# Both feed-forward up stages of a hybrid decoder layer: combined right blocks formed token-major in place, and the second norm's affine moved into the norm

## Chip, cores and metric

One core of a Trainium2 chip runs the whole layer. The metric is the device time of one execution in microseconds (us). The profile is of one execution; TensorE's clock is reported as a share of its full speed, the upper of its two levels (2.4 GHz); the other is 1.2 GHz.

## What is computed

The layer is a first feed-forward block (f1), a token mixer (retention and RWKV-7 heads), a second feed-forward block (f2) and a gated embedding, each of the first three followed by a residual sum and a layer norm. All of it is fp32, for 1024 tokens of width 1024; the hidden width D_FF is 2816.

```python
def _layer_norm(x, g, b):
    xf = x.astype(jnp.float32)
    mu = jnp.mean(xf, axis=-1, keepdims=True)
    var = jnp.mean(jnp.square(xf - mu), axis=-1, keepdims=True)
    y = (xf - mu) * lax.rsqrt(var + LN_EPS) * g.astype(jnp.float32) + b.astype(jnp.float32)
    return y.astype(x.dtype)

def _swiglu(x, w_gu, w_down):
    hdn = jnp.einsum('bsd,df->bsf', x, w_gu)
    gate, up = jnp.split(hdn, 2, axis=-1)
    return jnp.einsum('bsf,fd->bsd', jax.nn.silu(gate) * up, w_down)

x = _layer_norm(DEEPNORM_ALPHA * x + 0.5 * _swiglu(x, ffn1_w_gu[i], ffn1_w_down[i]), ln1_g[i], ln1_b[i])
mix = _token_mixer(x, w_in[i], ret_gn_g[i], ...)
x = _layer_norm(DEEPNORM_ALPHA * x + mix, ln2_g[i], ln2_b[i])
x = _layer_norm(DEEPNORM_ALPHA * x + 0.5 * _swiglu(x, ffn2_w_gu[i], ffn2_w_down[i]), ln3_g[i], ln3_b[i])
```

## The kernel before

An fp32 matrix product is made from three products of rounded parts: a `hi` part (a cast to fp32r on ScalarE, ACT, line L47) and a `lo` part (source minus hi, on VectorE, DVE, or GpSimd, POOL, line L48). `mm3` issues them as L61, L62 and L63.

**The up stage** (`ffn_up`) multiplies x by w_gu, which gives the gate and the up half (two *parts*). Tokens and features are halved, which gives two-by-two blocks, and each part of each hidden slice j = 0 to 10 takes seven block products m1 to m7 (the table `PRODUCTS`) in place of eight, of 12 matmuls of 128x512 each: 84 matmuls to a part, 168 to a slice. The left operands are combinations S1 to S4 of the weight blocks A11 to A22, made anew for each j in `ffn_w`: load (`f1w`, `f2w`, L100, on SyncE's DMA queue, SP), sums on DVE (L107), splits on ACT with DVE or POOL. The right operands are the token blocks B11, B21, B22 and their combinations T1 = B12 - B11, T3 = B22 - B12, T2 = B22 - T1, T4 = B21 - T2. They are made once, while slice j = 0 runs, and stay in SBUF for the ten slices after it.

The tokens lie token-major. A matmul wants them feature-major, so TensorE transposes them by 128x128 pieces (L229, into a PSUM tile `tp` of which there are two). Before, the four plain blocks are transposed (64 transposes to a stage). B11 and B21 are split straight from there (`first`). Of the other two, c and d (tiles called `pair`), ACT copies the transposed block to SBUF (`place`, L234; in f2 with the affine of the second norm, gain and bias as columns, L236), and then T1, T3, T2 and T4 are formed feature-major from SBUF (`sub` and `add`, L224 and L178) and split (`store`, L240 and L224), on DVE and POOL. In the code j = 0 is written out by hand, products in the order 1, 2, 5, 7, 6, 3, 4; the scheduler of the framework then sets each engine's order by priorities and dependences.

**Weights of the down stage.** `down_blocks` loads four blocks of w_down for one f (`f1tb`, `f2tb`, L146), subtracts on POOL (L148) and stores the four results to DRAM (`wt`, L149), where the down stage fetches them. A call after slice j handles f = j - 1; the call after j = 1 also handles f = 10. These loads and stores share SP's queue with the weight loads of the next slices, in order.

**The second norm.** The mixer's last step, `w_out_group`, adds its products into eight token tiles `xacc` (L1133, DVE). `layer_norm_stats` takes statistics on DVE (L507, L508, L510, L511) and normalises a tile in one ACT instruction (L513). The first four tiles (h = 0) are normalised at the end of the mixer (L1193), ahead of the last group (L1194), the other four (h = 1) when f2's j = 0 first asks for them (`load2`, L1406). Gain and bias are put on twice: by `place` and the split in f2's j = 0, and again token-major in `ffn_down` on the residual (`affine`, 16 DVE instructions of 128x1024, with gain and bias loaded as rows, 512 KB each).

Of the kernel before, what the change touches and what calls it, by code (L numbers as in the profile page):

```python
# [29 lines left out]
class Layer:  # L30
# [120 lines left out]
    def ffn_up(self, nm, X, xp, pool, pp, load, pair, release, w_gu, hd, hooks, w_down, wt, gb=None):  # L151
# [69 lines left out]

        tmp = lambda: pool.tile([P, HALF], F32, tag="s", name=f"{nm}t{self.uid()}", bufs=5)
        part = lambda n, k: (X[n][0][:, k], X[n][1][:, k])
        sub = lambda eng, o, a, b: eng.tensor_tensor(out=o, in0=a, in1=b, op=ALU.subtract)  # L224

        def transposed(half, h, k):
            ps = pp.tile([P, HALF], F32, tag="tp", name=f"{nm}tp{h}_{k}", bufs=2)
            for j in range(4):
                nc.tensor.transpose(ps[:, j * P:(j + 1) * P], half[j][:, k * P:(k + 1) * P], self.ident)  # L229
            return ps  # L230

        def place(dst, ps, k):
            if gb is None:
                nc.scalar.copy(dst, ps)  # L234
            else:
                nc.scalar.activation(dst, ps, AF.Identity, bias=gb[1][:, k:k + 1], scale=gb[0][:, k:k + 1])  # L236

        def store(n, k, src, eng, copy=None):
            hi, lo = part(n, k)
            (copy or nc.scalar.copy)(hi, src)  # L240
            sub(eng, lo, src, hi)

        def first(n, kh):
            for k in range(4):
                ps = transposed(half, 0, kh + k)
                if gb is None:
                    store(n, k, ps, V)
                else:
                    t = tmp()
                    place(t, ps, kh + k)  # L250
                    store(n, k, t, G_ if k % 2 else V, V.tensor_copy)

        with ExitStack() as c1, ExitStack() as c2:
            half = load(0, 0)
            s = [start(0, p_, None, None) for p_ in range(2)]
            stage = lambda: [next(p_.g) for p_ in s]
            load(0, 1)
            half1 = load(1, 0) if gb is None else None
            stage()
            if half1:  # L260
                load(1, 1)
            first("B11", 0)
            stage()
            first("B21", 4)
            b = {}
# [5 lines left out]
            if not half1:  # L271
                half1 = load(1, 0)
            c, d = zip(*[pair(k) for k in range(4)])
            early = xp.tile([P, 4, HALF], F32, tag="T4l", name=nm + "T2")
# [12 lines left out]
            for p_ in s:  # L287
                b[5, p_] = matmuls(p_, 5)
# [51 lines left out]
            for j in range(1, NJ):  # L340
# [14 lines left out]
                for f in (j - 1, NJ - 1)[:1 + (j == 1)]:  # L355
# [1112 lines left out]
```

## Time and profile before

| what | value |
|---|---|
| median of three runs | 2406.56 us (2405.73 to 2412.31) |
| the profiled execution's own time | 2407.18 us |
| its span | 2405.4 us |
| mean granted clock | 0.975 |
| PE busy | 2262.6 us, 94% of the span |
| DVE busy | 1667.1 us, 69% |
| ACT busy | 823.1 us, 34% |
| POOL busy | 839.0 us, 35% |
| DMA | 345.96 MB, mean 144 GB/s |
| chain that ended last | PE 73%, DVE 18%, DMA 3%, issue 3%, ACT 2%, POOL 1% |

The span is the profiled time without what lies around it (1.8 us here). A busy share is a mean over stages: PE is close to full in most of the program, and DVE's 69% is the mean of stretches in which it is idle half the time and others in which it never stops. "Chain" is the sequence of work that ended last, followed backwards through what released each step.

### The profile page before, as it was taken

How to read it: one execution, taken by the hardware profiler on the slowest of the kernel's cores; microseconds unless marked ns; L12 is line 12 of the kernel's file. 1: busy time of each engine (PE TensorE's matmuls, PEld its weight loads, DVE VectorE, ACT ScalarE, POOL GpSimd, SP SyncE). 2: the span in 40 equal slices, each digit the busy share in tenths (PEclk: the TensorE clock that was granted, in tenths of full speed). 3: DMA queues.
4: the chain of work that ended last, by engine and by line, in shares of the span. 5: the costliest groups of instructions: out<-in, count | busy, mean ns of one | idle time of the engine just before them, and what ended most of it. 6: DMA issues, size and time to landing. Idle time of an engine off the chain costs nothing.

```text
span 2405.4 us, 30769 instructions
## 1 busy us (share of the span) xinstructions
PE 2262.6 (94%) x10705; PEld 1809.2 (75%) x10705; DVE 1667.1 (69%) x2688; ACT 823.1 (34%) x1398; POOL 839.0 (35%) x642
## 2 busy tenths in 40 slices
PE   7999999999998999999899899978999999999989
PEld 5778888788776677777677677756888887787767
DVE  7776877656783378774864866688677766867862
ACT  4322332244532523322322323263223322445430
POOL 4754454200223333332533433257545443001330
PEclk9999999999998999999999999998999999999999
DMA  3545445397335442333333353224554543974321
GB/s 110 180 153 168 151 156 167 124 352 240 98 114 164 153 121 88 105 85 105 112 97 103 112 170 116 85 88 140 184 162 141 175 141 129 379 244 132 97 75 40
DMA packets 289841, 345.96 MB, mean 144 GB/s; under 512 B 35571, under 2 KB 162134, under 8 KB 289686
## 3 DMA queue, kind: packets, MB, share of 16 engines
q1 hardware_dynamic: 286128, 335.04, 43.5%
q0 software_dynamic: 2304, 8.39, 0.9%
q8 instruction: 84, 1.38, 0.2%
q10 hardware_dynamic: 1254, 0.58, 0.1%
q14 instruction: 71, 0.58, 0.1%
HBM read 237.50 MB, written 106.43 MB: 143 GB/s over the span
## 4 chain that ended last, share of the span: by engine, by line
PE 73%; DVE 18%; DMA 3%; issue 3%; ACT 2%; POOL 1%; SPq 1%; ACTq 0%; DVEq 0%; POOLq 0%
PE f2m L63 5%; PE f2m L62 5%; PE f2m L61 5%; PE f1m L61 5%; PE f1m L62 5%; PE f1m L63 5%; PE z L62 3%; PE z L61 3%; PE z L63 3%; PE f1qa L62 2%; PE f1qa L63 2%; PE f1qa L61 2%; PE scpw L1041 1%; DVE ixw L977 1%; DVE itw L975 1%
## 5 line engine op out<-in xcount | busy, mean ns | idle before, releaser
L63 PE MATMUL z<-x1Th,lo_win 128*128 128x512 f32 x448 | 189.2, 422 | 3.5 <-DVE lo_win L48 2.9
L61 PE MATMUL z<-x1Th,hi_win 128*128 128x512 f32 x448 | 188.9, 422 | 0.5 <-ACT hi_win L47 0.5
L62 PE MATMUL z<-x1Tl,hi_win 128*128 128x512 f32 x448 | 187.0, 417 | 0.0
L48 POOL TENSOR_TENSOR lo_win<-raw_win,hi_win 128x512 fp32r<-128x512 f32 x54 | 75.4, 1396 | 156.7 <-ACT hi_win L47 136.9
L975 DVE TENSOR_TENSOR itw<-iltw,ixw 32x31 f32<-32x31 f32 (+15 forms) x248 | 106.7, 430 | 28.8 <-DMA iltw<-scrw 13.4
L977 DVE TENSOR_TENSOR ixw<-ixw,itw 32x31 f32<-32x31 f32 (+15 forms) x248 | 109.7, 442 | 4.0
L63 PEld LDWEIGHTS z<-x1Th,lo_win 128*128 128x128 f32 x448 | 86.8, 194 | 23.3 <-DVE lo_win L48 3.8
L61 PEld LDWEIGHTS z<-x1Th,hi_win 128*128 128x128 f32 x448 | 86.6, 193 | 22.7 <-issue 3.6
L62 PEld LDWEIGHTS z<-x1Tl,hi_win 128*128 128x128 f32 x448 | 86.9, 194 | 19.8 <-issue 3.0
L148 POOL TENSOR_TENSOR f2tb<-f2tb,f2tb 128x512 f32<-128x512 f32 x44 | 68.3, 1553 | 76.6 <-DMA f2tb<-in_ffn_w_down 69.3
L148 POOL TENSOR_TENSOR f1tb<-f1tb,f1tb 128x512 f32<-128x512 f32 x44 | 67.1, 1526 | 70.5 <-DMA f1tb<-in_ffn_w_down 65.5
L48 DVE TENSOR_TENSOR f1hl<-f1s,f1hh 128x512 fp32r<-128x512 f32 x63 | 44.9, 713 | 61.4 <-ACT f1hh L47 59.8
L48 DVE TENSOR_TENSOR f2hl<-f2s,f2hh 128x512 fp32r<-128x512 f32 x63 | 44.7, 710 | 47.9 <-ACT f2hh L47 47.8
L107 DVE TENSOR_TENSOR f2S<-f2w 128x512 f32<-128x512 f32 x22 | 17.5, 794 | 82.2 <-DMA f2w<-in_ffn_w_gu 82.2
L62 PE MATMUL f2qa<-f2vl,f2hh 128*128 128x512 f32 x164 | 65.0, 397 | 3.6 <-DVE f2vl L48 3.6
L62 PE MATMUL f1qa<-f1vl,f1hh 128*128 128x512 f32 x164 | 64.6, 394 | 3.1 <-DVE f1vl L48 3.1
L47 ACT CAST f2hh<-f2s 128x512 fp32r<-128x512 f32 x63 | 39.2, 623 | 82.2 <-PE f2qb L62 35.3
L47 ACT CAST f1hh<-f1s 128x512 fp32r<-128x512 f32 x63 | 39.2, 622 | 80.7 <-PE f1qa L62 35.3
L47 ACT CAST hi_win<-raw_win 128x512 fp32r<-128x512 f32 x56 | 34.6, 618 | 93.8 <-PE z L62 83.6
L601 ACT COPY zs<-z 128x512 f32<-128x512 f32 x56 | 32.7, 583 | 95.6 <-PE z L63 80.2
L107 DVE TENSOR_TENSOR f1S<-f1w 128x512 f32<-128x512 f32 x22 | 16.2, 738 | 70.6 <-DMA f1w<-in_ffn_w_gu 60.6
L63 PE MATMUL f2qa<-f2vh,f2hl 128*128 128x512 f32 x164 | 64.5, 393 | 0.5 <-DVE f2hl L48 0.5
(791 smaller groups left out, 7314.9 us busy)
## 6 DMA issues: line engine op xcount, KB each, us to landing
f1w<-in_ffn_w_gu SPq DMA_DIRECT2D x44, 512.0 KB
f2w<-in_ffn_w_gu SPq DMA_DIRECT2D x44, 512.0 KB
f1s<-hd SPq DMA_DIRECT2D x63, 256.0 KB
f2s<-hd SPq DMA_DIRECT2D x63, 256.0 KB
zs<-zs SPq DMA_DIRECT2D x56, 256.0 KB
raw_win<-in_w_in SPq DMA_DIRECT2D x54, 256.0 KB
f1tb<-in_ffn_w_down SPq DMA_DIRECT2D x44, 256.0 KB
wt<-f1tb SPq DMA_DIRECT2D x44, 256.0 KB
```

What stands on the lines that cost most here:

```text
L47: self.last_split = self.nc.scalar.copy(hi, src).ins
L48: (eng or self.nc.vector).tensor_tensor(out=lo, in0=src, in1=hi, op=ALU.subtract)
L61: mm(ps, a[0], b[0], start=first, stop=False)
L62: mm(ps, a[0], b[1], start=False, stop=False)
L63: mm(ps, a[1], b[0], start=False, stop=last)
L107: sub = lambda o, a, b, op=ALU.subtract: V.tensor_tensor(out=o, in0=a, in1=b, op=op)
L148: nc.gpsimd.tensor_tensor(out=t, in0=a, in1=b, op=ALU.subtract)
L601: nc.scalar.copy(zs, ps)
L975: nc.vector.tensor_tensor(out=t, in0=lt[:, j, j + 1:].unsqueeze(2).broadcast_to([B, n, c]), in1=x[:, j:j + 1, 0:c].broadcast_to([B, n, c]) ...
L977: nc.vector.tensor_tensor(out=x[:, j + 1:, 0:c], in0=x[:, j + 1:, 0:c], in1=t, op=ALU.add)
L1041: nc.tensor.matmul(ps[e][:, 0:2 * P], kp[rr, cs], ar[rr, c].rearrange("p a t -> p (a t)"), start=True, stop=True)
```

## The change

In `ffn_up` the combinations are formed before the transposes, token-major and in place in the tiles that hold the tokens (a, b, c and d are the slices with B11, B12, B21 and B22): a becomes T1 = b - a on DVE, b becomes T3 = d - b on POOL, d becomes T2 = d - a on DVE once B22 has been transposed, and c becomes T4 = c - d on POOL. Each of the seven right blocks then goes through the new function `block`: 16 transposes, hi by ACT and lo by DVE, both straight from PSUM. That is 112 transposes to a stage for 64, no `pair`, and no affine in f2's up stage. The products are called in the order 1, 2, 5, 7, 6, 3, 4 as before. Over the program DVE has 2606 rows before and after, ACT 1411 and 1395, POOL 641 and 627, PE 8964 and 9060.

`layer_norm_stats` gets an optional pair of rows; with them it normalises and applies gain and bias in four DVE instructions of 128x512 to a tile (L471 and L476 in the new numbering) and no ACT one. All eight tiles go this way at the end of the mixer; the rows lie in two matrices of the mixer (`M1`) that are free by then. `ffn_down` loses its 16 affine instructions and two loads. `down_blocks` is called for f = j - 2, not after j = 1, and twice after j = 4 (f = 2 and 9) and j = 7 (f = 5 and 10).

```diff
@@ ffn_up
+        cut = lambda tiles, n: [t[:, n * HALF:(n + 1) * HALF] for t in tiles]
+        def subs(eng, out, x, y):
+            for o, p, q in zip(out, x, y):
+                eng.tensor_tensor(out=o, in0=p, in1=q, op=ALU.subtract)
+        def block(n, src):
+            for k in range(4):
+                ps = pp.tile([P, HALF], F32, tag="tp", name=f"{nm}tp{n}_{k}", bufs=2)
+                for i in range(4):
+                    nc.tensor.transpose(ps[:, i * P:(i + 1) * P], src[i][:, k * P:(k + 1) * P], self.ident)
+                self.split(X[n][0][:, k], X[n][1][:, k], ps)
...
-            for k in range(4):
-                place(c[k], transposed(half1, 1, k), k)
-                t = early[:, k]
-                sub(V, t, c[k], part("B11", k)[0])
-                sub(V, t, t, part("B11", k)[1])
-                store("T1", k, t, G_)
+            subs(V, a, b, a)
+            block("T1", a)
             for p_ in s:
-                b[2, p_] = matmuls(p_, 2)
-            for k in range(4):
-                place(d[k], transposed(half1, 1, 4 + k), 4 + k)
-            load(1, 2)
+                r[2, p_] = matmuls(p_, 2)
+            subs(G_, b, d, b)
             stage()
             for p_ in s:
-                b[5, p_] = matmuls(p_, 5)
+                r[5, p_] = matmuls(p_, 5)
+            block("T3", b)
+            stage()
+            block("B22", d)
+            for p_ in s:
+                r[7, p_] = matmuls(p_, 7)
+            subs(V, d, d, a)
+            block("T2", d)
+            subs(G_, c, c, d)
...
-            for k in range(4):
-                sub(V, c[k], d[k], c[k])
-                store("T3", k, c[k], V)
...
-            for k in range(4):
-                t = early[:, k]
-                sub(V, t, d[k], t)
-                store("T2", k, t, V)
             for p_ in s:
-                b[6, p_] = matmuls(p_, 6)
...
-                sub(G_, c[k], part("B21", k)[0], early[:, k])
...
-                add(c[k], c[k], part("B21", k)[1], V)
-                store("T4", k, c[k], G_)
+                r[6, p_] = matmuls(p_, 6)
+            block("T4", c)
...
-                for f in (j - 1, NJ - 1)[:1 + (j == 1)]:
+                for f in {1: (), 4: (2, 9), 7: (5, 10)}.get(j, (j - 2,)):
                     self.down_blocks(nm, w_down, wt, f, pool)
...
@@ ffn_down
-        def affine(t):
-            V.tensor_tensor(out=acc[t], in0=acc[t], in1=gb[1][0], op=ALU.mult)
-            V.tensor_tensor(out=acc[t], in0=acc[t], in1=gb[1][1], op=ALU.add)
...
@@ layer_norm_stats
+        if rows:
+            for i in range(2):
+                a = x[:, i * HALF:(i + 1) * HALF]
+                nc.vector.scalar_tensor_tensor(out=a, in0=a, scalar=mv[:, 0:1], in1=rows[0][i], op0=ALU.subtract, op1=ALU.mult)
         nc.vector.reciprocal(mv[:, 3:4], mv[:, 2:3])
+        if rows:
+            for i in range(2):
+                a = slice(i * HALF, (i + 1) * HALF)
+                nc.vector.scalar_tensor_tensor(out=out[:, a], in0=x[:, a], scalar=mv[:, 3:4], in1=rows[1][i],
+                                               op0=ALU.mult, op1=ALU.add)
+            return
...
@@ mixer
-            normalise(mb)
+            gb = []
+            for e, t in zip("gb", self.M1):
+                r = t.rearrange("p s j -> p (s j)")
+                nc.sync.dma_start(r, self.A[f"ln2_{e}"].broadcast_to([P, D]))
+                gb.append((r[:, :HALF], r[:, HALF:]))
+            normalise(0, mb, gb)
             self.w_out_group((7, 3), mixed, (1,))
+            normalise(1, mb, gb)
```

DVE in f1's j = 0, around the blocks T3 and T2 (`pair` and `f1T` are SBUF tiles, `f1tp` is a PSUM tile, `x` a token tile, `f1w` and `f1S` weights), before:

```order
L224 TENSOR_TENSOR f1T3l_93<-pair4_232,f1T3h_92 128x512
L224 TENSOR_TENSOR pair5_233<-pair5_233 128x512
L224 TENSOR_TENSOR pair6_234<-pair6_234 128x512
L107 TENSOR_TENSOR f1w1_0_107<-f1S11_0_332,f1w1_0_107 128x512
L224 TENSOR_TENSOR f1T2_235<-pair3_231,f1T2_235 128x512
L224 TENSOR_TENSOR f1T3l_93<-pair5_233,f1T3h_92 128x512
L224 TENSOR_TENSOR f1T3l_93<-pair6_234,f1T3h_92 128x512
L224 TENSOR_TENSOR f1T2_235<-pair4_232,f1T2_235 128x512
L48 TENSOR_TENSOR f1S2l0_0_434<-f1w0_0_105,f1S2h0_0_433 128x512
L48 TENSOR_TENSOR f1S2l1_0_439<-f1w1_0_107,f1S2h1_0_438 128x512
L224 TENSOR_TENSOR f1T2l_89<-f1T2_235,f1T2h_88 128x512 x2
L224 TENSOR_TENSOR f1T2_235<-pair5_233,f1T2_235 128x512
```

and with the change:

```order
L48 TENSOR_TENSOR f1B22l_83<-f1tpB22_2_383,f1B22h_82 128x512
L228 TENSOR_TENSOR x4_113<-x4_113,x0_97 128x512
L48 TENSOR_TENSOR f1B22l_83<-f1tpB22_3_390,f1B22h_82 128x512
L228 TENSOR_TENSOR x5_114<-x5_114,x1_98 128x512
L228 TENSOR_TENSOR x6_115<-x6_115,x2_99 128x512
L228 TENSOR_TENSOR x7_116<-x7_116,x3_100 128x512
L48 TENSOR_TENSOR f1S2l0_1_648<-f1w0_1_631,f1S2h0_1_647 128x512
L107 TENSOR_TENSOR f1S11_1_781<-f1w1_12_771 128x512
L48 TENSOR_TENSOR f1T2l_89<-f1tpT2_0_427,f1T2h_88 128x512
L48 TENSOR_TENSOR f1T2l_89<-f1tpT2_1_434,f1T2h_88 128x512
L107 TENSOR_TENSOR f1w1_12_771<-f1w1_1_769,f1w1_12_771 128x512
L48 TENSOR_TENSOR f1T2l_89<-f1tpT2_2_441,f1T2h_88 128x512
```

The subtractions that formed T3 and T2 piece by piece between their splits are gone from here; the splits read `f1tp`, DVE keeps the four subtractions of T2, ahead of all four of its splits, and weight work of slice 1 stands among them.

DVE where the norm meets f2's first right block (`lnstln` statistics, `M10` and `M11` gain and bias), before:

```order
L1133 SCALAR_TENSOR_TENSOR xacc7_11770<-wopo7_1_1_3_13245,xacc7_11770 128x512
L511 SCALAR_TENSOR_TENSOR lnstln24_13411<-lnstln24_13411 128x1
L508 BN_AGGR lnstln25_13419<-lnstln25_13419 128x2
L507 BN_STATS lnstln26_13427<-xacc6_11769 128x6 x2
L240 CAST f2B11h_13270<-f2t187_13298 128x512
L240 CAST f2B11h_13270<-f2t188_13307 128x512
L224 TENSOR_TENSOR f2B11l_13271<-f2t187_13298,f2B11h_13270 128x512
L48 TENSOR_TENSOR f2A11l0_0_13330<-f2w0_0_13281,f2A11h0_0_13329 128x512
L240 CAST f2B11h_13270<-f2t189_13316 128x512
L240 CAST f2B11h_13270<-f2t190_13325 128x512
```

and with the change:

```order
L471 SCALAR_TENSOR_TENSOR xacc6_11806<-xacc6_11806,lnstln26_13320,M10_6325 128x512 x2
L472 RECIPROCAL lnstln26_13320<-lnstln26_13320 128x1
L466 BN_AGGR lnstln27_13330<-lnstln27_13330 128x2
L476 SCALAR_TENSOR_TENSOR xacc6_11806<-xacc6_11806,lnstln26_13320,M11_6326 128x512 x2
L471 SCALAR_TENSOR_TENSOR xacc7_11807<-xacc7_11807,lnstln27_13330,M10_6325 128x512 x2
L472 RECIPROCAL lnstln27_13330<-lnstln27_13330 128x1
L476 SCALAR_TENSOR_TENSOR xacc7_11807<-xacc7_11807,lnstln27_13330,M11_6326 128x512 x2
L48 TENSOR_TENSOR f2B11l_13358<-f2tpB11_0_13380,f2B11h_13357 128x512
L48 TENSOR_TENSOR f2B11l_13358<-f2tpB11_1_13387,f2B11h_13357 128x512
L228 TENSOR_TENSOR xacc0_11800<-xacc4_11804,xacc0_11800 128x512
```

Before, B11's splits stood among the statistics of the last tiles; now the last tile's normalisation and affine stand ahead of the first split.

SP's queue in f1 around the weight loads of slice 2 (`f1w0_2`, `f1w0_13`, `f1w1_2`, `f1w1_13`; the digit before the underline is the part), before:

```order
L146 DMA f1tb10_0_892<-in_ffn1_w_down 128x512
L146 DMA f1tb10_1_893<-in_ffn1_w_down 128x512
L146 DMA f1tb10_2_894<-in_ffn1_w_down 128x512
L146 DMA f1tb10_3_895<-in_ffn1_w_down 128x512
L100 DMA f1w0_2_910<-in_ffn1_w_gu 128x8x128
L149 DMA wt_67<-f1tb10_0_892 128x512
L149 DMA wt_67<-f1tb10_1_893 128x512
L149 DMA wt_67<-f1tb10_2_894 128x512
L149 DMA wt_67<-f1tb10_3_895 128x512
L100 DMA f1w0_13_912<-in_ffn1_w_gu 128x8x128
L100 DMA f1w1_2_1048<-in_ffn1_w_gu 128x8x128
L100 DMA f1w1_13_1050<-in_ffn1_w_gu 128x8x128
```

and with the change:

```order
L100 DMA f1w1_1_769<-in_ffn1_w_gu 128x8x128
L100 DMA f1w1_12_771<-in_ffn1_w_gu 128x8x128
L100 DMA f1w0_2_915<-in_ffn1_w_gu 128x8x128
L100 DMA f1w0_13_917<-in_ffn1_w_gu 128x8x128
L214 DMA hd_66<-f1G0_463 128x3x512
L219 DMA hd_66<-f1U0_464 128x4x512
L100 DMA f1w1_2_1053<-in_ffn1_w_gu 128x8x128
L100 DMA f1w1_13_1055<-in_ffn1_w_gu 128x8x128
L146 DMA f1tb0_0_1197<-in_ffn1_w_down 128x512
L146 DMA f1tb0_1_1198<-in_ffn1_w_down 128x512
```

The loads of two sets of `f1tb` (f = 0, not shown, and f = 10) and most of their stores stood ahead of slice 2's weight loads; now the first two of those four loads follow slice 1's directly, and the first set comes behind all four.

## Rows read from the trace of the kernel before

**Rows 1.** The page's busy times of the whole span.

```profile
PE 2262.6 (94%) x10705; PEld 1809.2 (75%) x10705; DVE 1667.1 (69%) x2688; ACT 823.1 (34%) x1398; POOL 839.0 (35%) x642
```

**Rows 2.** Timeline of PE (start us, us, line, operation): first matmul of each part.

```profile
73.47 0.39 PE L61 MATMUL f1m<-f1B11h,f1A11h 128*128 128x512 f32 x1
...
97.12 0.39 PE L61 MATMUL f1m<-f1B11h,f1A11h 128*128 128x512 f32 x1
...
116.31 0.50 PE L61 MATMUL f1m<-f1B11h,f1A11h 128*128 128x512 f32 x1
...
141.07 0.79 PE L61 MATMUL f1m<-f1B11h,f1A11h 128*128 128x512 f32 x1 [3.65 <-DVE f1G L178]
...
162.66 0.39 PE L61 MATMUL f1m<-f1B11h,f1A11h 128*128 128x512 f32 x1
...
1581.24 0.49 PE L61 MATMUL f2m<-f2B11h,f2A11h 128*128 128x512 f32 x1
...
1650.10 0.39 PE L61 MATMUL f2m<-f2B11h,f2A11h 128*128 128x512 f32 x1
...
1679.07 0.39 PE L61 MATMUL f2m<-f2B11h,f2A11h 128*128 128x512 f32 x1
...
1698.11 0.39 PE L61 MATMUL f2m<-f2B11h,f2A11h 128*128 128x512 f32 x1
```

**Rows 3.** Windows: start:end, us, busy (x instructions) of PE, PEld, DVE, ACT, POOL; clock, DMA.

```profile
40.00:60.00 20.00, 12.73 (x36) 8.96 (x37) 20.00 (x21) 8.50 (x16) 11.89 (x9) 0.77 0.03 9
...
80.00:100.00 20.00, 16.70 (x74) 13.52 (x73) 12.29 (x15) 4.98 (x10) 19.84 (x11) 1.00 0.41 147
...
1640.00:1660.00 20.00, 15.24 (x63) 10.99 (x61) 20.00 (x21) 8.28 (x12) 15.38 (x10) 1.00 0.46 141
```

**Rows 4.** PE's waits: us, times, longest; windows 0:74, 74:160 and 1660:1760.

```profile
PE f1m L62 <- DVE f1T3l L224: 3.9, 2, 3.4
...
PE f1m L63 <- POOL f1S3l L48: 3.3, 1, 3.3
...
PE f2m L63 <- DVE f2S2l L48: 5.3, 1, 5.3
```

**Rows 5.** The chain that ended last, between 60 and 160 us (start us, us, what).

```profile
108.00 1.29 POOL f1tb L148
...
109.68 4.46 DMA f1w<-in_ffn_w_gu
114.24 0.70 DVE f1S L107
...
141.87 0.43 PE f1m L62
```

**Rows 6.** Timeline of DVE and POOL in f1's j = 0.

```profile
39.00 3.44 DVE L224 TENSOR_TENSOR pair<-pair 128x512 f32<-128x512 f32 x2
...
63.69 1.27 DVE L178 TENSOR_TENSOR f1t<-f1m,f1t 128x512 f32<-128x512 f32 x2
...
61.47 3.46 POOL L224 TENSOR_TENSOR f1T4l<-pair,f1T4h 128x512 fp32r<-128x512 f32 x2
```

**Rows 7.** Timeline of PE: eight transposes, and the first matmul of m5 in either stage.

```profile
27.27 1.04 PE L229 MATMUL f1tp<-ident,x 128*128 128x128 f32 x8
28.06 0.48 PE L61 MATMUL f1m<-f1T1h,f1S1h 128*128 128x512 f32 x1
...
1607.39 0.74 PE L61 MATMUL f2m<-f2T1h,f2S1h 128*128 128x512 f32 x2 [0.38 <-ACT f2T1h L240]
```

**Rows 8.** DVE by lines, 1553.8 to 1580.7 us (busy, mean ns, idle before), then its timeline.

```profile
L1133 DVE SCALAR_TENSOR_TENSOR xacc<-wopo,xacc 128x512 f32<-128x512 f32 x17 | 11.6, 687 | 3.6 <-PE wopo L63 3.2
L507 DVE BATCH_NORM_STATS2 lnstln<-xacc 128x6 f32<-128x512 f32 x14 | 9.3, 683 | 1.3 <-ACT xacc L513 1.2
...
1581.23 0.68 DVE L224 TENSOR_TENSOR f2B11l<-f2t,f2B11h 128x512 fp32r<-128x512 f32 x1
```

**Rows 9.** PE's waits in f2's down stage, 2040 to 2210 us.

```profile
PE f2qa L62 <- DVE f2vl L48: 0.5, 1, 0.5
```

More of the change, by code (lines that the diff above doesn't have):

```diff
@@ L222, in ffn_up @@
         tmp = lambda: pool.tile([P, HALF], F32, tag="s", name=f"{nm}t{self.uid()}", bufs=5)
[L223 to L243, printed above, removed]
-            for k in range(4):
[L245 to L251, printed above, removed]
+        cut = lambda tiles, n: [t[:, n * HALF:(n + 1) * HALF] for t in tiles]
[3 more added lines that the diff above has]
+        def block(n, src):
+            for k in range(4):
+                ps = pp.tile([P, HALF], F32, tag="tp", name=f"{nm}tp{n}_{k}", bufs=2)
+                for i in range(4):
+                    nc.tensor.transpose(ps[:, i * P:(i + 1) * P], src[i][:, k * P:(k + 1) * P], self.ident)
+                self.split(X[n][0][:, k], X[n][1][:, k], ps)
         with ExitStack() as c1, ExitStack() as c2:
             half = load(0, 0)
+            a, c = cut(half, 0), cut(half, 1)
             s = [start(0, p_, None, None) for p_ in range(2)]
@@ L257, in ffn_up @@
             load(0, 1)
-            half1 = load(1, 0) if gb is None else None
+            half = load(1, 0)
+            b, d = cut(half, 0), cut(half, 1)
             stage()
-            if half1:
-                load(1, 1)
-            first("B11", 0)
+            load(1, 1)
+            block("B11", a)
             stage()
-            first("B21", 4)
-            b = {}
+            block("B21", c)
+            r = {}
             for p_ in s:
@@ L270, in ffn_up @@
             stage()
[L271 to L274, printed above, removed]
-            for k in range(4):
-                place(c[k], transposed(half1, 1, k), k)
-                t = early[:, k]
-                sub(V, t, c[k], part("B11", k)[0])
-                sub(V, t, t, part("B11", k)[1])
-                store("T1", k, t, G_)
+            load(1, 2)
+            subs(V, a, b, a)
+            block("T1", a)
             for p_ in s:
-                b[2, p_] = matmuls(p_, 2)
-            for k in range(4):
-                place(d[k], transposed(half1, 1, 4 + k), 4 + k)
-            load(1, 2)
+                r[2, p_] = matmuls(p_, 2)
+            subs(G_, b, d, b)
             stage()
             for p_ in s:
-                b[5, p_] = matmuls(p_, 5)
+                r[5, p_] = matmuls(p_, 5)
[7 more added lines that the diff above has]
+            subs(G_, c, c, d)
             release(1)
@@ L294, in ffn_up @@
                 p_.V = v
-                add(v[:, 0], b[2, p_], p_.p1)
-                nc.scalar.copy(v[:, 1], b[5, p_])
-            for k in range(4):
-                sub(V, c[k], d[k], c[k])
-                store("T3", k, c[k], V)
+                add(v[:, 0], r[2, p_], p_.p1)
+                nc.scalar.copy(v[:, 1], r[5, p_])
+                nc.scalar.copy(v[:, 2], r[7, p_])
             stage()
-            for k in range(4):
-                store("B22", k, d[k], G_)
             for p_ in s:
-                ps = matmuls(p_, 7)
-                nc.scalar.copy(p_.V[:, 2], ps)
+                r[6, p_] = matmuls(p_, 6)
+            block("T4", c)
             stage()
-            for k in range(4):
-                t = early[:, k]
-                sub(V, t, d[k], t)
-                store("T2", k, t, V)
             for p_ in s:
-                b[6, p_] = matmuls(p_, 6)
-            X["T4"] = tuple(xp.tile([P, 4, HALF], F32R, tag="T4" + e, name=nm + "T4" + e) for e in "hl")
-            for k in range(4):
-                sub(G_, c[k], part("B21", k)[0], early[:, k])
-            stage()
-            for k in range(4):
-                add(c[k], c[k], part("B21", k)[1], V)
-                store("T4", k, c[k], G_)
-            for p_ in s:
-                ps = b[6, p_]
+                ps = r[6, p_]
                 v = p_.V
@@ L466, in mid1 @@
                 load_acc(4 + f - 3)
-            if f == 3 and gb:
-                self.affine_rows(*gb)
-            if gb and f > 6:
-                affine(4 + f - 7)
         def mid5(f):
@@ L474, in mid5 @@
                 load_acc(f - 1)
-            if gb and f in (4, 6, 8, 10):
-                affine((f - 4) // 2)
         b = product(1, "a", mid1)
@@ L499, in uid, with layer_norm_stats @@
         return self._uid
-    def layer_norm_stats(self, t, x, out, pool, eps):
+    def layer_norm_stats(self, t, x, out, pool, eps, rows=None):
         nc = self.nc
@@ L1314, in up, with down @@
                     hooks = {4: lambda ep: L.load_params(ep, pp, L.marks["f1", "4_0"])} if nm == "f1" else {}
[L1315 to L1317 removed]
+                    L.ffn_up(nm, X, xp, wp, pp, lambda h, n: load(h, n, xp), release, w_gu, hd, hooks, w_down, wt)
+        def down(nm, ln, w_down, x, xT, fp, ap, dst, more):
             acc = [ap.tile([P, D], F32, tag=f"acc{t}", name=f"{nm}acc{t}") for t in range(TT)]
@@ L1357, in down @@
                 tr(1, "a")
-                if xln:
-                    gb = [fp.tile([P, D], F32, tag=f"ln{e}r", name=f"{nm}{e}r2") for e in "gb"]
                 L.affine_rows(ln, gb)
```

29 lines of the change are left out of this document (11 added, 18 removed).

## The prediction

> **What bounds the kernel now.** I read four views in this order. The page's busy times [rows 1] show PE at 94% and DVE at 69%: as a mean, the kernel is bound by TensorE, so a change to other engines can pay only where PE waits. The timeline of PE at the first matmul of each part [rows 2] shows where. A part that nothing holds up takes 1698.11 - 1679.07 = 19.04 us (84 matmuls at 0.227). In f1, slice 1 and slice 2 take 23.65, 19.19, 24.76 and 21.59 us for their four parts, together 13.0 over 4 x 19.04. In f2 the first part of slice 1 takes 28.97, 9.9 over, and later ones nothing over. Slice 0 of either stage has 168 matmuls, 38.1 us, but takes over 60. The windows [rows 3] show who is full there: from 40 to 60 and from 1640 to 1660 DVE is busy for all 20.00 us, and PE only for 12.73 and 15.24; from 80 to 100 it is POOL, with 19.84. The waits of PE [rows 4] name the same: the T3 split on DVE in slice 0, `f1S3l` on POOL and `f2S2l` on DVE in slice 1. So two places can move: slice 0 of both stages (DVE-bound) and slices 1 and 2, which pay for what DVE, POOL and SP carry over.
>
> **The change, part by part.** All sums are against the profiled execution, 2407.18 us, which lies 0.6 above the median of the runs.
>
> *Transposes.* 48 more to a stage. Eight take 1.04 us [rows 7], so 48 take 6.2 us a stage. They lie in a stretch where PE waits for DVE, and are hidden as long as it does; without that cover they cost 6.2 each stage. The Trainium skill ("VectorE: DVE Perf Modes", The three transpose paths) gives 390 ns for one TensorE transpose of 128x128 in bf16; by it these 48 would be 18.7 us a stage. The row of this trace, fp32, has 0.13 us each in a run, and the measurement decides.
>
> *Slice 0 of f1.* Until about 19 us nothing differs. T1 no longer waits for an ACT copy and the eight transposes ahead of m5 move, so m5 begins at about 27.0 where it began at 28.06 [rows 7]. DVE then has ten weight operations before the T3 splits. One 128x512 operation follows another after 0.60 us alone, and after 1.7 when both inputs are in SBUF and POOL works (two take 3.44, [rows 6]). I take a mixed 1.2, so the last T3 split is done at about 42, and m7 ends at about 47, after a stretch in which PE has been idle 5 us and runs at its lower clock (0.43 us from matmul to matmul, [rows 5]). B22's four splits, three weight operations and the four subtractions of T2, which now all stand before T2's first split, take another 13 us; with T2's splits m6 begins at 56 to 57. m6, m3 and m4 are 3 x 24 x 0.227 = 16.3 us, and I add 3.5 for slow clock and T4: slice 1 begins at 76.5, against 73.47 [rows 2]. **+3.** All operations at 0.60 would give -7, all at 1.7 give +8; I stand between, nearer the slow end because POOL is busy for 11.89 of 20 us there [rows 3].
>
> *Slices 1 and 2 of f1.* The chain [rows 5] runs POOL's `f1tb` subtraction (to 109.3), the weight load behind it (4.46 us), and DVE's S1 at 114.24, which slice 2 needs. With the change these loads no longer stand behind two sets of `f1tb`, POOL has no set to subtract in slice 1, and the S3 and S2 splits are ahead of slice 1 in their queues. Of the 13.0 us I take back 12, since one set remains in slice 2. **-12**, bounds -13 and -5 (the wait on `f1S3l` alone, 3.3, and its slow clock).
>
> *Start of f2.* The norm of all eight tiles stands before the first B11 split on DVE. From 1553.8 to 1580.7 DVE now does 17 additions and 14 statistics [rows 8], 31 operations. With the change it is 17 + 16 + 32 = 65, at 0.60 us 39.0; 16 small ones add 2.5 (each 0.2 or less) and early waits on PE some 2. 1553.8 + 43.5 = 1597.3, against 1581.23 [rows 8]: 16.1 later. PE idles for most of that. From there DVE has 22 operations up to the end of T1, 13 to 22 us by the two prices; since T1's first blocks are enough, m5 begins at about 1612, where it was 1607.39 [rows 7]: the norm of tiles 4 to 7 and the ACT copies that stood between are gone. From m5 to slice 1 I take f1's walk, 76.5 - 27.0 = 49.5, in place of 42.7: 1661.5 to 1662, against 1650.10. **+12**, bounds +6 (T1 done at 13 us and DVE less hindered by POOL) and +19 (the whole 16.1, and 3 as in f1).
>
> *Slice 1 of f2.* The wait on `f2S2l` is one of DVE backlog [rows 4]; in the new order that split stands among slice 0's work, ahead of T2's. The 9.9 goes but for the slow clock and one wait on POOL. **-9**, bounds -9.9 and 0.
>
> *Second sets after slices 4 and 7.* The same work as after slice 1 before, which cost f1 part of its 13.0 and f2 nothing after slice 1 (1679.07 to 1698.11 is a full-speed part, [rows 2]). Here nothing else is late. **+2** for four of them, bounds 0 and +8.
>
> *The rest.* 16 affine operations and 1 MB of loads leave f2's down stage. PE waits for a DVE split there for 0.5 us [rows 9]. **-0.5**; the cover of the rest is PE itself. The two loads of gain and bias move into the mixer; a load of that size takes 4.46 us [rows 5], stands early in SP's queue, and nothing waits for it before the norm: 0, with 4.5 as its upper bound. ACT's 16 and POOL's 14 operations less are on engines that are idle for over 60% of the span [rows 1]; that POOL has fewer is part of the prices above.
>
> Sum: 3 - 12 + 12 - 9 + 2 - 0.5 = -4.5, so 2402.7 for an execution like the profiled one, and **2402** against the median. That is **no change** within 0.3% (7.2 us, about what a measurement of this kernel can tell from none): what slices 1 and 2 win, f2's start gives back.
>
> **The rivals.** *Faster: DVE escapes POOL.* In [rows 6] two operations with both inputs in SBUF take 3.44 us while POOL works, but two that read one input from PSUM take 1.27 beside a POOL operation. In slice 0, 20 block operations of DVE change from the first kind to the second; if 12 of them stood beside POOL, that is 12 x 1.1 = 13 us of DVE time a stage in a DVE-bound stretch, and POOL has 8 operations fewer to hinder with. If 9 to 10 us of it reaches PE, f1's slice 0 turns from +3 to -6 and f2's start from +12 to +4: the sum is -6 - 12 + 4 - 9 + 2 - 0.5 = -21.5, that is 2385. The Trainium skill ("GPSIMD Engine Reference", Specifications) says POOL's SBUF interfaces are shared with VectorE and contend with instructions that have two SBUF inputs; by that rule this rival follows, and the trace agrees with the rule. Against it speaks that the T2 subtractions and the weight sums keep two SBUF inputs, and that the order puts them in front of the splits that PE waits for.
>
> *Slower: the norm holds f2.* If PE's wait for the norm is not made up in slice 0 (+19) and DVE is then so late that `f2S2l` still holds slice 1 (0 in place of -9), the sum is 3 - 12 + 19 + 0 + 2 - 0.5 = +11.5, that is 2418. It decides where slice 1 of f2 begins after 1668. For it speaks that 32 added operations stand in one piece before the only split that PE can begin with; against it that the work they replace stood on the same path.
>
> *The gain does not come:* the second sets after slices 4 and 7 hold SP's queue and POOL as the two after slices 0 and 1 did, four times. At 3 us each that is +12 in place of +2, and the sum is +5.5, 2412, the upper end of no change.
>
> **How the numbers follow.** No change, with the last rival in it, has 0.42, and its own range is 2399.3 to 2413.8. Faster has 0.36: the first rival with 0.24, and 0.12 for my sum with the low ends of two terms. Slower has 0.22: the second rival with 0.14, and 0.08 for high ends of the terms. The range runs from 2387 to 2417; some 0.1 of the chance is left out at either end.
>
> **What would show it.** First matmuls of a part at: f1 slice 1 at 76.5 (right within 4), then four parts of 19.1 to 20; f2 slice 1 some 12 later than before counted from the last `wopo` matmul's old place, with a first part under 20.5. DVE should run without a gap from 1564 to 1597, and PE be idle for over 10 us before m1 of f2. Parts after slices 4 and 7 should stay within 1 us of 19.04. The prediction is wrong if slice 0 of f1 ends before 70 (the first rival), if f2's slice 1 begins after 1668 on the old scale (the second), or if slices 1 and 2 keep waits of over 5 us.

## The result and the profile after

The change makes the kernel **slower** by 0.7%: 2425.47 us median of 9 runs (2413.48 to 2430.92) against 2406.56 of 9 (2402.24 to 2412.31), ratio 1.007 [1.005, 1.0091]. The prediction, 2402 with a range of 2387 to 2417, was wrong. The profiled execution took 2417.59 us (span 2415.7, mean granted clock 0.969), 10.4 more than that of before; the places below account for it.

The page's busy times, against [rows 1]: PE has 13 us more, DVE 16 and POOL 55 less. By these means nothing got worse. The profile counts 24 instructions less on ACT, 20 less on POOL and 4 more on DVE; the 16, 14 and none that the prediction and the section on the change go by are not its counts.

```profile
PE 2275.9 (94%) x10801; PEld 1825.4 (76%) x10801; DVE 1651.5 (68%) x2692; ACT 809.1 (33%) x1374; POOL 784.1 (32%) x622
```

PE's timeline at the first matmul of slices 1 and 2 of f1, of f2 itself, and of f2's slice 1 (both parts), against [rows 2]:

```profile
80.80 0.39 PE L61 MATMUL f1m<-f1B11h,f1A11h 128*128 128x512 f32 x1
99.83 0.39 PE L61 MATMUL f1m<-f1B11h,f1A11h 128*128 128x512 f32 x1
...
1603.01 0.79 PE L61 MATMUL f2m<-f2B11h,f2A11h 128*128 128x512 f32 x1 [0.34 <-ACT f2A11h L47]
...
1672.76 0.39 PE L61 MATMUL f2m<-f2B11h,f2A11h 128*128 128x512 f32 x1
1691.80 0.39 PE L61 MATMUL f2m<-f2B11h,f2A11h 128*128 128x512 f32 x1
```

Slice 1 of f1 begins 7.3 us later than before, but the parts of the two slices behind it are at full speed (19.03 to 19.05). f2 begins 21.8 us later and its slice 1 22.7, and the first part of that is 19.04 as well. From such starts, in the two profiles:

| place | predicted | measured |
|---|---|---|
| f1 slice 0 | +3 | +7.5 |
| f1 slices 1 and 2 | -12 | -13.0 |
| f1's start (-0.2) and slices 4 and 5 (-3.9; before, PE waited there 2.1 us on a DMA and had the lower clock for 3.4) | not in the sum | -4.1 |
| f1's down stage and the mixer up to f2 | 0 | +10.6 |
| start and slice 0 of f2 | +12 | +21.6 |
| f2 slice 1 | -9 | -9.9 |
| second sets after slices 4 and 7 | +2 | 0 |
| the rest | -0.5 | -2.4 |
| sum | -4.5 | +10.3 |

PE's waits in the first 90 us, and below them those from 1553 to 1680 (total, count, longest), against [rows 4]: `f1S3l` and `f2S2l` are gone, and T2 and the first B11 split have come.

```profile
PE f1m L61 <- ACT f1T3h L47: 3.9, 1, 3.9
PE f1tpT L235 <- DVE f1T2l L48: 3.9, 2, 3.3
PE f1tpT L235 <- DVE x L228: 2.6, 4, 1.1
...
PE f2tpB L235 <- DVE f2B11l L48: 13.0, 1, 13.0
PE f2tpT L235 <- DVE f2T2l L48: 3.9, 2, 3.3
PE f2m L61 <- ACT f2T3h L47: 3.4, 1, 3.4
```

*f1, slice 0.* PE's timeline between m7 and m6 shows why m6 begins so late. It began at 52.0 before, right behind m7. Now m7 ends at 47.6, about as forecast, but all 16 transposes of T2 stand ahead of m6 in PE's queue. They need the four subtractions (`x`, L228) and share two PSUM tiles, so the third block can't be transposed before the first is split.

```profile
56.07 1.97 PE L235 MATMUL f1tpT<-ident,x 128*128 128x128 f32 x8 [3.25 <-DVE f1T2l L48]
58.68 1.09 PE L235 MATMUL f1tpT<-ident,x 128*128 128x128 f32 x4 [0.64 <-DVE f1T2l L48]
59.42 0.78 PE L61 MATMUL f1m<-f1T2h,f1S2h 128*128 128x512 f32 x1
```

DVE's timeline has what they wait for. Three subtractions take 3.65 us (both inputs in SBUF, POOL at work for most of it), and a weight split and a weight sum of 1.75 each stand between them and the T2 splits, which read PSUM and take 0.64 each (POOL is done by then):

```profile
48.43 3.65 DVE L228 TENSOR_TENSOR x<-x,x 128x512 f32<-128x512 f32 x3
...
52.00 1.75 DVE L48 TENSOR_TENSOR f1S2l<-f1w,f1S2h 128x512 fp32r<-128x512 f32 x1
53.67 1.75 DVE L107 TENSOR_TENSOR f1S<-f1w 128x512 f32<-128x512 f32 x1
55.34 1.28 DVE L48 TENSOR_TENSOR f1T2l<-f1tpT,f1T2h 128x512 fp32r<-128x512 f32 x2
```

*f2's start.* The windows (start:end, length, then busy time and count of PE, PEld, DVE, ACT and POOL, granted clock, DMA share, GB/s) show DVE full up to the first split at 1599.96, with PE busy for 7.12 of 20 us. Then PE is busy for 18.22 of 20 us, at 0.82 of its clock:

```profile
1580.00:1600.00 20.00, 7.12 (x32) 5.25 (x32) 19.95 (x39) 2.14 (x6) 2.13 (x4) 0.75 0.26 105
1600.00:1620.00 20.00, 18.22 (x86) 14.96 (x87) 18.79 (x27) 11.02 (x20) 10.38 (x8) 0.82 0.26 79
```

What DVE does from 1554.8 to 1599.9 (its lines in that stretch):

```profile
L1101 DVE SCALAR_TENSOR_TENSOR xacc<-wopo,xacc 128x512 f32<-128x512 f32 x17 | 11.4, 681 | 2.0 <-PE wopo L63 1.9
L471 DVE SCALAR_TENSOR_TENSOR xacc<-xacc,lnstln,M 128x512 f32<-128x512 f32 x16 | 11.3, 744 | 0.0
L476 DVE SCALAR_TENSOR_TENSOR xacc<-xacc,lnstln,M 128x512 f32<-128x512 f32 x16 | 11.3, 746 | 0.0
L465 DVE BATCH_NORM_STATS2 lnstln<-xacc 128x6 f32<-128x512 f32 x16 | 10.6, 680 | 0.1
```

*The mixer.* Up to 1396 the changed kernel is 8.5 us ahead, at 1424 it is 0.8 behind. The same window of both, before first, does not hold quite the same matmuls; what differs is the granted clock, 0.83 and 0.50 (the lower level for the whole stretch), while PE was busy for all 20.00 us:

```profile
1400.00:1420.00 20.00, 17.19 (x100) 13.04 (x99) 14.02 (x33) 2.28 (x5) 4.14 (x4) 0.83 0.26 79
```

```profile
1400.00:1420.00 20.00, 20.00 (x71) 13.98 (x71) 8.12 (x25) 2.28 (x5) 1.15 (x2) 0.50 0.20 67
```

The medians differ by 18.9 us, more than the two profiles. In the runs of each kernel a longer time goes with a lower mean granted clock, with the change by about 2 us per 0.001 (2413.48 at 0.970 and 2430.92 at 0.962), with the kernel before by 0.9 to 1.7. The profiled execution was one of its faster ones.

### The profile page after: what moved, and what is told of

It is laid out like the page before. It is cut to its first block, busy times and chain, and to the rows that moved or that the text cites. A ratio compares the mean times of both kernels' runs of the same rounds, so it can differ in the third digit from the quotient of the medians.

```text
span 2415.7 us, 30928 instructions
## 1 busy us (share of the span) xinstructions
PE 2275.9 (94%) x10801; PEld 1825.4 (76%) x10801; DVE 1651.5 (68%) x2692; ACT 809.1 (33%) x1374; POOL 784.1 (32%) x622
## 4 chain that ended last, share of the span: by engine, by line
PE 76%; DVE 17%; issue 2%; ACT 2%; DMA 2%; POOL 1%; SPq 0%; DVEq 0%; ACTq 0%; POOLq 0%
PE f1m L62 6%; PE f1m L61 6%; PE f1m L63 6%; PE f2m L61 5%; PE f2m L62 5%; PE f2m L63 5%; PE z L63 3%; PE z L61 3%; PE z L62 3%; DVE ixw L945 2%; DVE itw L943 2%; PE scpw L1009 2%; PE f1qa L62 1%; PE f1qa L61 1%; PE f1qa L63 1%
## 5 line engine op out<-in xcount | busy, mean ns | idle before, releaser
L61 PE MATMUL f2qa<-f2vh,f2hh 128*128 128x512 f32 x164 | 64.5, 395 | 0.0
L48 POOL TENSOR_TENSOR f1A12l<-f1w,f1A12h 128x512 fp32r<-128x512 f32 x22 | 31.6, 1437 | 99.6 <-ACT f1A12h L47 99.6
```

The lines of the kernel that those rows point to most:

```text
L48: (eng or self.nc.vector).tensor_tensor(out=lo, in0=src, in1=hi, op=ALU.subtract)
L61: mm(ps, a[0], b[0], start=first, stop=False)
```

## Experiments

Three questions: what took the waits out of slices 1 and 2 (the new table of sets, or the right blocks); what costs the 21.6 us at f2's start and the 7.5 in f1 (the norm's place, the place of T2, or only clock); and whether the slow stretch in the mixer belongs to the change.

### The two parts of the change alone

**sets_only**: the kernel before with one line of the change.

```diff
-                for f in (j - 1, NJ - 1)[:1 + (j == 1)]:
+                for f in {1: (), 4: (2, 9), 7: (5, 10)}.get(j, (j - 2,)):
```

> The kernel before with nothing changed but the table of slices after which sets of w_down are prepared (f = j - 2, two sets after slices 4 and 7). Theory (the stalls of slices 1 and 2 come from the sets' place, the norm and slice 0 are what the change loses by): f1's slices 1 and 2 fall from 13.0 us over full speed to under 3, f2's first part of slice 1 from 28.97 to under 22, slice 0 of both stages stays within 1 us (62.97 and 68.86), and the time falls by 15 to 23 us, to 2384 to 2392. Rival (those stalls go because the right blocks no longer load DVE and POOL): slices 1 and 2 keep over 8 of the 23 us, and the time falls by less than 12.

Measured: 2396.32 us (2390.76 to 2401.05, 5 runs; before 2407.7 in this series), ratio 0.995 [0.9931, 0.9968]: faster than both kernels. First matmuls of slice 1 and of its second part in f1, then the same in f2:

```profile
72.85 0.39 PE L61 MATMUL f1m<-f1B11h,f1A11h 128*128 128x512 f32 x1
98.12 0.39 PE L61 MATMUL f1m<-f1B11h,f1A11h 128*128 128x512 f32 x1
...
1644.71 0.39 PE L61 MATMUL f2m<-f2B11h,f2A11h 128*128 128x512 f32 x1
1668.57 0.39 PE L61 MATMUL f2m<-f2B11h,f2A11h 128*128 128x512 f32 x1
```

The first parts still take 25.27 and 23.86 us, and PE still waits 3.3 us for `f1S3l` and 1.9 for `f2S2l`. What follows: the rival was right. Against the first profile of before the table alone gives 6.8 of f1's 13.0 us and 5.1 of f2's 9.9. The size for f1 is not firm: the second profile of before (before_again, below) has parts of 26.23, 19.04, 20.91 and 19.17 us there, 9.2 over full speed, and against it the table gives 3.0 (in f2 4.9 of 9.7).

**sets_back**: the change with the old table (the same lines, signs turned).

> The changed kernel with the old table of sets (f = j - 1, and f = 10 after slice 1). Theory (sets): f1's slices 1 and 2 lose 8 to 13 us again, the rest stays, and the time rises by 8 to 20 us over the changed kernel. Rival (right blocks): the slices keep within 3 us of full speed, and the time stays within 5 us of the changed kernel.

Measured: 2420.72 us (2418.97 to 2426.59, 4 runs), ratio 1.0054 [1.0038, 1.007]. f1's slice 1 begins at 79.66, and the two parts behind it have these starts:

```profile
98.70 0.39 PE L61 MATMUL f1m<-f1B11h,f1A11h 128*128 128x512 f32 x1
117.74 0.39 PE L61 MATMUL f1m<-f1B11h,f1A11h 128*128 128x512 f32 x1
```

All parts of slices 1 and 2 take 19.04 us with the old table too. So the rival was right: the right blocks alone are enough, and beside them the table changes nothing in these slices (slice 4's second part takes 20.75 us for the change's 19.08). Nor do these slices run freely only because slice 0 got longer: with t2_t3's order (below) slice 0 takes 64.09 us, and they still take 19.04 a part. The prediction had put f1's gain down to the sets for the most part, and f2's to the new order of the splits.

**no_affine**: the change without gain and bias in the norm (the 32 added DVE instructions fall away, and ACT normalises again; the two loads of rows stay, unused).

```diff
-                L.layer_norm_stats(f"ln2{t}", L.xacc[t], L.xacc[t], pool, eps, gb)
+                L.layer_norm_stats(f"ln2{t}", L.xacc[t], L.xacc[t], pool, eps)
```

> The changed kernel without the second norm's gain and bias: each tile is normalised in one ACT instruction, and the 32 DVE instructions go (the two loads of rows stay). Theory (32 operations of 0.66 us stand in one chain before f2's first product): the first product of f2 comes 15 to 21 us earlier than in the changed kernel, slice 0 of f2 stays within 4 us of 69.75, and the time falls by 12 to 22 us. Rival (DVE is the bound up to the end of slice 0 anyway, so that an earlier start is lost again there): the first product comes earlier, slice 0 becomes longer by over 8, and the time falls by less than 8.

Measured: 2407.51 us (2394.2 to 2415.75, 10 runs), ratio 0.999 [0.997, 1.001]. First matmul of f2 and of its slice 1:

```profile
1581.57 0.79 PE L61 MATMUL f2m<-f2B11h,f2A11h 128*128 128x512 f32 x1 [0.34 <-ACT f2A11h L47]
...
1649.87 0.39 PE L61 MATMUL f2m<-f2B11h,f2A11h 128*128 128x512 f32 x1
```

f2 begins 21.4 us earlier than in the change. Some 7 of these are the mixer's slow stretch, which this execution did not have, so about 14 are the affine in the norm, about as the theory had it (15 to 21). Slice 0 of f2 takes 68.3 us, hardly less than in the change (69.75): once it begins, it has much the same walk. From the first of the mixer's last 96 `wopo` matmuls to slice 1 of f2 it is 97.3 us before, 119.0 with the change and 103.5 here: of the 21.6 us, 15.5 are gain and bias in the norm, and 6.1 the rest, the norm of all eight tiles ahead of the first split among it.

**change_again**: the changed kernel once more.

> The changed kernel once more, unaltered, for a second profile. Theory (the 9.3 us that the mixer lost between 1400 and 1425 us came from a stretch in which TensorE was granted its lower clock, and where such stretches fall differs from run to run): the mixer loses another amount, between 0 and 9 us, with slow stretches elsewhere, while f1's slices and f2's start repeat within 1.5 us. Rival (the loads of gain and bias, or a changed order, hold the mixer there): the loss of 8 to 10 us comes at the same place.

Measured: 2421.35 us (2416.71 to 2425.96, 4 runs), ratio 1.0052 [1.0033, 1.0072]. f1's slice 0 takes 71.98 us, f2 begins at 1603.33: the waits in the up stages repeat. The slow stretch does not stay in its place, but from the end of f1's up stage to the last 96 `wopo` matmuls this profile loses as much against before as the first (9.4 and 10.6 us), so neither the theory nor its rival came out whole:

```profile
1400.00:1420.00 20.00, 18.28 (x117) 14.16 (x118) 14.60 (x39) 3.07 (x8) 1.98 (x3) 1.00 0.38 127
1420.00:1440.00 20.00, 19.82 (x102) 16.85 (x101) 12.58 (x39) 5.67 (x14) 6.00 (x7) 0.70 0.65 233
```

### Orders that take the waits away

**t2_in_a**: T2 = B22 - T1 is written over T1's tokens by POOL, ahead of m5, so that the transposes of T2 don't wait for DVE's subtractions.

```diff
             subs(G_, b, d, b)
+            subs(G_, a, d, a)
...
-            subs(V, d, d, a)
-            block("T2", d)
-            subs(G_, c, c, d)
+            block("T2", a)
+            subs(G_, c, c, a)
```

> The changed kernel, but T2 = d - a is written over a (free once T1 has been transposed) by POOL and ahead of m5, not over d by DVE after B22's transposes. Theory (slice 0 grew because T2 cannot begin before B22's transposes and then needs all four subtractions at once, while weight work stands between): slice 0 of f1 falls from 70.5 to 63 to 66 us and that of f2 by 2 to 5 us, the time by 6 to 12 us. Rival (slice 0 grew through the 48 added transposes and the two PSUM tiles that hold them): slice 0 of f1 stays over 68.5, the time within 4 us.

Measured: 2413.23 us (2403.53 to 2422.24, 10 runs; before 2405.75 in this series), ratio 1.0019 [0.9995, 1.0042]. f1's slice 0 takes 66.77 us (-3.7) and f2's 64.91 (-4.8). m6 now begins at 55.7, right behind m7, but m7 is later: its wait for `f1T3h` grew from 3.9 to 10.3 us.

```profile
PE f1m L61 <- ACT f1T3h L47: 10.3, 1, 10.3
```

ACT stands there behind the split of `f1S4h`, and that behind DVE's weight sums. POOL, which now forms T2 too and T4 earlier, is busy here from 22.8 to 47.3 us without a pause, and beside it DVE's weight operations from 33 to 41.6 take 1.7 us each; in the change POOL is idle from 31.9 to 36.1, and they take 0.7 there:

```profile
41.67 0.62 ACT L47 CAST f1S4h<-f1w 128x512 fp32r<-128x512 f32 x1 [6.06 <-DVE f1w L107]
```

**t2_t3**: and `block("T3", b)` ahead of that weight work.

```diff
             subs(G_, b, d, b)
+            block("T3", b)
             subs(G_, a, d, a)
...
-            block("T3", b)
```

> As t2_in_a, and T3's transposes and splits stand ahead of the weight work that m5 is followed by, so that ACT casts T3 before S2, S4 and A22. Theory (PE's 3.9 us wait before m7 is ACT's order): that wait falls under 1 us, slice 0 of f1 comes to 60 to 63 us, 2 to 4 below t2_in_a. Rival (m7 then waits for S3, or m6 for S2, by as much): slice 0 within 1 us of t2_in_a.

Measured: 2408.24 us (2401.11 to 2418.8, 10 runs), ratio 1.0007 [0.9989, 1.0025]. f1's slice 0 takes 64.09 us, 2.7 below t2_in_a and near before's 62.97, and f2's 66.23, 1.3 above it. The wait for `f1T3h` is gone; the transposes of T3 now wait 5.1 us for the T3 splits on DVE.

**late_norm**: the change, but the norm of tiles 4 to 7 with its affine is called from f2's slice 0, behind the B21 splits (`late` holds the two rows, loaded once more; the edits for that are left out here).

```diff
-            normalise(1, mb, gb)
...
+            if h == 1 and n == 0:
+                normalise2(1, xp, late["gb"])
```

> The changed kernel with the norm of tiles 4 to 7 behind the splits of B11 and B21 (rows of gain and bias loaded once more, into the tile that T4's lo part takes later). Theory (the loss at f2's start is that B11 and B21, which need only tiles 0 to 3, stand behind the norm of all eight; DVE's added work counts less): f2's first product comes 10 to 14 us earlier than in the changed kernel, slice 0 of f2 grows by 4 to 8, the end of it comes 4 to 9 us earlier. Rival (DVE has the same work up to T1, so all of it comes back): the end of slice 0 within 2 us of the changed kernel. Third (TensorE is never idle for 13 us, and keeps its clock): the end comes over 10 us earlier.

Measured: 2415.41 us (2411.7 to 2420.46, 10 runs), ratio 1.0032 [1.0019, 1.0045].

```profile
1591.39 0.50 PE L61 MATMUL f2m<-f2B11h,f2A11h 128*128 128x512 f32 x1 [0.77 <-ACT f2A11h L47]
...
1667.42 0.39 PE L61 MATMUL f2m<-f2B11h,f2A11h 128*128 128x512 f32 x1
```

f2 begins 11.6 us earlier, and its slice 0 takes 76.03 us, 6.3 more: half of what the earlier start won comes back as waits of T1's transposes (`xacc`, 8.1 us). DVE's work is moved, not saved.

**late_t2_t3**: both of these.

> late_norm and t2_t3 together. Theory (the two losses are apart, and add): the sum of both gains within 3 us, a time of 2396 to 2406, slices 1 and 2 without a stall. Rival (both draw on the same DVE backlog): less than two thirds of the sum.

Measured: 2405.55 us (2395.94 to 2412.53, 10 runs), ratio 0.9986 [0.9969, 1.0003]. By the medians late_norm gives 10.1 us and t2_t3 17.2 against the first 2425.47 (5.9 and 13.1 against change_again), together 19.9 (15.8). That is over two thirds of the sum, so the rival is out, but 3 to 7 us short of the sum; with runs of one kernel 9 to 18 us apart, whether the two overlap is not shown. With all of it the change is as fast as the kernel before, not faster.

### The mixer's slow stretch, and the best version

**f1_change**: f1's up stage and the table as in the change; norm, mixer and f2 as before.

```diff
+            if nm == "f1":
+                L.ffn_up_new(...)
+            else:
+                L.ffn_up(...)
```

> The first stage as the change has it (right blocks token-major) with the new table of sets, and the norm and the second stage as before. Theory (in f1 the change wins: slice 0 costs 7, slices 1 and 2 and the wait in slice 4 give back 17): the last part of f1 begins 8 to 11 us earlier than before, f2's first product too, slice 0 of f2 stays at 68.9, its slice 1 keeps some 5 us of stall, and the time falls by 10 to 17 us against before. Rival (the mixer takes it back, as it did with the whole change): f2's first product comes less than 4 us earlier, and the time is within 5 us of before.

Measured: 2406.3 us (2398.43 to 2415.41, 10 runs; before 2407.31), ratio 0.9993 [0.9975, 1.0011]. No affine norm and no loads of gain and bias are in this mixer, and still the profiled execution has the slow stretch, in the same place. Its f1 ends 9.3 us earlier than before, as forecast, but f2 begins 7.3 later, and the median moves by 1 us: the rival came. Four of its ten runs lie at 2398 to 2400 with a mean clock of 0.975 or 0.976, the others at 2405 to 2415 with 0.969 to 0.972.

```profile
1400.00:1420.00 20.00, 20.00 (x66) 13.79 (x64) 8.70 (x27) 2.28 (x5) 1.14 (x2) 0.50 0.14 43
```

**hybrid**: f1_change with t2_t3's order in f1.

> As f1_change, with T2 written over a and T3 ahead of the weight work in f1. Theory (the gains add): slice 0 of f1 at 64 to 65.5, the time 15 to 23 us below before, 4 to 9 below sets_only (2396). Rival: within 3 us of sets_only.

Measured: 2401.29 us (2391.12 to 2412.62, 12 runs), ratio 0.9973 [0.9954, 0.9992]. Slice 0 of f1 takes 63.94 us, about as forecast, but the time misses both theory and rival: it is 6 us below before and 5 above sets_only. The profiled execution, at 2392.82 one of its fastest, has the full clock in the window:

```profile
1400.00:1420.00 20.00, 20.00 (x123) 15.43 (x122) 13.90 (x41) 4.70 (x13) 2.58 (x5) 1.00 0.53 174
```

Its interval overlaps that of sets_only; which of the two is faster is open.

**change_third** and **before_again**, one profile each of the changed kernel and of the kernel before.

> The changed kernel a third time. Theory (where TensorE's clock falls in the mixer differs from run to run): between 1340 and 1450 us the slow time is not that of either profile had so far (27 us at 1395; 7 at 1360 and 14 at 1428), while slice 0 of f1 stays at 70 to 72 and f1's later slices at 19.04. Rival: 27 us at 1395 again.

> The kernel before once more. Theory (the same chance holds for it): the slow time between 1340 and 1450 us lies between 7 and 30 us and need not be the 14 us of its first profile, slices 1 and 2 of f1 and f2 show the same stalls (13 and 9.9 us, within 2). Rival (the kernel before has no such stretch): 14 us again.

Measured: 2415.03 and 2412.2 us. Both rivals came: the changed kernel has its slow stretch again (27.3 us from 1393, as in the first profile); before has 13.6 us at the lower clock between 1330 and 1480, as in its first one. Of before's stalls in slices 1 and 2 f2's repeat (9.7 us), f1's are 9.2 in place of 13.0. From the end of f1's up stage to the last 96 `wopo` matmuls before_again takes 6.8 us more than before, so that the mixer's +10.6 has a spread of that size. Slice 0 of f1 takes 69.29 us and 63.5.

```profile
1400.00:1420.00 20.00, 20.00 (x67) 14.00 (x65) 8.14 (x25) 1.70 (x4) 1.15 (x2) 0.50 0.27 78
```

In that stretch the lower clock lasted 3.4 to 17.0 us in six of the profiles (before twice, sets_only, hybrid, t2_in_a, no_affine) and 23.9 to 40.9 in eight (the change three times, sets_back, t2_t3, late_norm, late_t2_t3, f1_change). So neither the affine norm nor its loads are needed for a long stretch (f1_change has neither), and kernels with both can have less of it (t2_in_a). The three profiles with the old right blocks in f1 are all among the six, and eight of the eleven with the new ones among the others. That leans towards f1's change, also in kernels whose mixer is that of before (f1_change, but not hybrid); what makes the stretch last, and whether the change makes it likelier, was not settled.

## Why the prediction was wrong

- **Start of f2, the term that was mis-sized: +12 predicted, +21.6 measured.** The walk of the norm was nearly right: first B11 split at 1599.96, 1.0 of it from upstream, against 1597.3. One added instruction follows the other after 0.66 us, for 0.60 in the text (from its start to its end one takes 0.745), and DVE ran without a gap from 1564. The step that failed is the next, "m5 begins at about 1612". It counted only DVE's 22 operations up to the end of T1. But PE had idled for 13.0 us, and its own m1 and m2 with 32 transposes, partly at the lower clock, take 17.5 us from 1603.01 (it is busy for 16.75 of them, at 0.88 of its clock), so m5 begins at 1620.5, though T1's first split is done at 1615.2. The rest of slice 0 takes 52.3 us where 49.5 was taken from f1's walk. no_affine and late_norm show where it comes from: without gain and bias 15.5 of the 21.6 us go, and half of what late_norm wins by moving half of the norm behind the first splits is lost again in slice 0. Slice 1 begins after 1668 on the old scale, which is the sign that the slower rival named; but its other half did not come, since the wait on `f2S2l` went.
- **Slice 0 of f1: +3 predicted, +7.5 measured.** m7 ended at 47 as the walk had it. The step that failed is "with T2's splits m6 begins at 56 to 57": it put the splits in DVE's order and left out that PE's queue holds all T2 transposes ahead of m6 with two PSUM tiles for them: m6 began at 59.4. From there to slice 1 it took 21.4 us, 1.6 more than the sum had. t2_in_a took this wait away, and showed the one behind it (ACT at T3), which t2_t3 took away in turn. The faster rival's premise, that operations reading PSUM escape POOL, held where the two stand side by side: beside the same POOL work two T1 splits, from PSUM, took 1.29 us and two weight splits, from SBUF, 3.34 (the rows below). But the subtractions and weight operations in front of the T2 splits did not escape it (1.2 in the mean and 1.75), and POOL was idle when the T2 splits ran.

```profile
21.48 1.29 DVE L48 TENSOR_TENSOR f1T1l<-f1tpT,f1T1h 128x512 fp32r<-128x512 f32 x2
22.68 3.34 DVE L48 TENSOR_TENSOR f1S1l<-f1S,f1S1h 128x512 fp32r<-128x512 f32 x2
...
21.05 6.13 POOL L228 TENSOR_TENSOR x<-x 128x512 f32<-128x512 f32 x4 [5.63 <-DMA x<-in_x]
```

- **Slices 1 and 2: -12 and -9 predicted, -13.0 and -9.9 measured.** The sizes were right (f1's is 9.2 against before_again); for f1 the cause was half wrong: the right blocks alone do it (sets_back), the table alone gives 3.0 to 6.8 (sets_only). For f2 it was right that `f2S2l` no longer waits in DVE's backlog. POOL reaches `f1S3l` while slice 0 still runs, at 65.22 for 1.29 us.
- **The mixer: 0 predicted, +10.6 measured**, 9.3 of it from 1396 to 1424. The prediction had put this term at nothing, with 4.5 for the loads of gain and bias as its bound. A stretch of lower clock that differs between profiles of one kernel was in no term; f1_change shows it without these loads. Its cause is open.
- **Second sets, the rest:** +2 and -0.5 predicted, 0 and -2.4 measured. f1's slices 4 and 5 gave 3.9 that no step had: there PE no longer waits for a DMA.

With terms of +7.5 and +21.6 in place of +3 and +12 the same sum would have been +9.6, or 2416. That this is near the profiled 2417.59 is luck: the mixer's +10.6 and the -9.9 by which the other terms were off cancel. The rest of the way to 2425 goes with the lower mean clock of its runs (0.966 in the mean, 0.973 in the later runs of before).

## What to carry to other kernels

When an engine is added to at the start of a stage, follow the queue of the engine that waits, too: once released, it still has its own work to do, at a clock that it lost while it idled (here 0.88 of full speed for 17.5 us, behind a wait of 13.0). An operation that is cheaper does not help if it stands behind a dearer one, or if its transposes stand as one block ahead of a product with two PSUM tiles between them. Try the parts of a change alone: here one line of it (sets_only) was worth more than the whole.

## What was unexpected of the hardware

One kernel's mean granted clock lay between 0.962 and 0.970 from run to run, which goes with 17 us of time. A stretch of over 20 us at the lower level came with PE busy for all of it (20.00 of 20 us), right behind a pause of PE of 1.9 to 2.0 us, in two of three profiles of the changed kernel; in hybrid and t2_in_a the same pause was followed by 6.8 us at that level. Two DVE operations of 128x512, one behind the other, took 1.28 us with both inputs in SBUF while POOL was idle, 3.34 beside POOL (two weight splits), and 1.29 beside POOL with one input in PSUM (two T1 splits); two of the norm's, with two SBUF inputs and a scalar per partition, took 1.41 with POOL busy for 2.13 of 20 us.
